# Gate and up of four feed-forward steps by one level of Strassen's algorithm, positions on partitions

## The chip, the core and the metric

The kernel runs on one core of one Trainium2 chip. The metric is the device time of one execution in microseconds (us). A core has TensorE (PE, matrix products, with its weight loads shown apart as PEld), VectorE (DVE), ScalarE (ACT), GpSimd (POOL) and SyncE (SP, which here only issues DMAs). Each engine works through its own instructions in order; they wait for one another on semaphores.

## The reference

Two layers of a decoder trunk on x of 512 positions by 1024 channels, all in float32. A layer is a feed-forward half step, a mixer, and a second feed-forward half step; a last norm ends it.

```python
def rmsnorm(x, g):                       # D_MODEL 1024, SEQ 512, D_FF 2816, DEPTH 2
    y = xf * lax.rsqrt(jnp.mean(xf * xf, axis=-1, keepdims=True) + RMS_EPS)
    return (y * g.astype(jnp.float32)).astype(x.dtype)
def swiglu(h, wg, wu, wd):
    return (jax.nn.silu(h @ wg) * (h @ wu)) @ wd
...
    for l in range(DEPTH):
        x = x + 0.5 * swiglu(rmsnorm(x, ffn1_norm[l]), ffn1_w_gate[l], ffn1_w_up[l], ffn1_w_down[l])
        x = x + hybrid_mixer(rmsnorm(x, mix_norm[l]), w_in[l], w_out[l], ...)
        x = x + 0.5 * swiglu(rmsnorm(x, ffn2_norm[l]), ffn2_w_gate[l], ffn2_w_up[l], ffn2_w_down[l])
    return rmsnorm(x, final_norm)
```

The mixer projects the normed x to 6168 columns, runs an mLSTM, a state-space scan and a convolution module on them, and projects 2048 columns back. Its computation is the same in both kernels.

## The kernel before

Activations lie with channels on partitions: x is eight tiles `xT` of 128 channels by 512 positions. A float32 product is made of three float32r passes. Each operand is split into a high part (a cast on ScalarE) and a low part (operand minus high part, on VectorE), and TensorE multiplies high by high, high by low and low by high. For weights this is `split_w` (L138; cast L145, difference L146, 128x1024 at a time, three buffers `whi` and three `wlo`), for activations `split_a` (L149; L151, L152). The normed input is the split pair `xh`, `xl` (eight tiles each), with the gain in it; the statistic R (one over the root of the mean square, a row of 512 repeated on all partitions) is multiplied in afterwards.

A feed-forward step `ffn` (L270) goes through its 2816 hidden columns in six groups, the first of 256 columns and five of 512. In a group each tile of 128 columns of gate, then of up, is a `proj` (L163): eight channel tiles by three passes, 24 matmuls with the weights stationary and 512 positions moving. An evicting chain follows: gate times R (L286), SiLU (L287), up times R (L288), their product (L289), and `split_a`. After the group's two or four hidden tiles, `contraction` (L236) multiplies them with the rows of the down weights into eight tiles of 128 channels, each added to `xT` (L263). In its first two output tiles the last hidden tile's part comes last.

Weights come by DMAs on SP's queue into three `raw` buffers of 1 MB (`stream`, L127). Mixers and feed-forward steps keep their own buffers at the same time. The order of each engine's instructions is set by a scheduler that takes them by priority, which is the place in the program's text; `shifted` moves a piece earlier or later in it (`early`: weights' loads and splits 100 steps ahead). Within an engine, what stands earlier is done earlier, whether or not what stands behind it could go first.

Between phases, `Norm.finish` (L216) makes R: column sums by TensorE (L188), root on ScalarE (L173), reciprocal on VectorE (L174), four transposes on TensorE (L181) and a copy (L220). In the first phase of all, R and the first products come from code of its own. The last contraction of the kernel is in `Final` (from L851), with positions on partitions; it transposes `xT` by L867.

## Time and profile before

| | us |
|---|---|
| median of 3 runs | 2321.57 (2321.07 to 2323.57) |
| span of the profiled execution | 2319.0 |
| TensorE busy in it | 2300.8 (99%) |
| VectorE busy | 1434.7 (62%) |
| ScalarE busy | 957.4 (41%) |
| moved by DMA | 224.64 MB, 97 GB/s |

The profiled execution's own device time is not listed apart from its span; the median of the runs is 2.6 us above that span, and this is taken as what lies around it. Matmuls overlap in the records: one lasts 0.39 us there, but the next starts some 0.23 us later, and this spacing is what a matmul costs while TensorE has no other wait. The same holds in a smaller measure on VectorE, where an instruction of 1.22 us lets the next begin after 1.14 us.

### The profile page before, as it was taken

How to read it: one execution, taken by the hardware profiler on the slowest of the kernel's cores; microseconds unless marked ns; L12 is line 12 of the kernel's file. 1: busy time of each engine (PE TensorE's matmuls, PEld its weight loads, DVE VectorE, ACT ScalarE, POOL GpSimd, SP SyncE). 2: the span in 40 equal slices, each digit the busy share in tenths (PEclk: the TensorE clock that was granted, in tenths of full speed). 3: DMA queues.
4: the chain of work that ended last, by engine and by line, in shares of the span. 5: the costliest groups of instructions: out<-in, count | busy, mean ns of one | idle time of the engine just before them, and what ended most of it. 6: DMA issues, size and time to landing. Idle time of an engine off the chain costs nothing.

```text
span 2319.0 us, 26273 instructions
## 1 busy us (share of the span) xinstructions
PE 2300.8 (99%) x10499; PEld 1893.0 (82%) x10499; DVE 1434.7 (62%) x2085; ACT 957.4 (41%) x1449; POOL 83.3 (4%) x145
## 2 busy tenths in 40 slices
PE   8999999999999999999999999999999999999998
PEld 7888888788888888888888888878888888888887
DVE  5444447999957654444554444489998586544445
ACT  5222225756555532222332222266666554222223
POOL 0000000010110000000000000000101000000000
PEclk9999999999999999999999999999999999999999
DMA  5232232333322322332323233323333323223231
GB/s 165 92 109 92 94 106 76 109 91 109 95 95 81 108 91 86 97 109 76 107 91 109 76 107 98 102 75 110 110 98 106 94 70 110 91 91 104 79 109 55
DMA packets 186010, 224.64 MB, mean 97 GB/s; under 512 B 5625, under 2 KB 147353, under 8 KB 185889
## 3 DMA queue, kind: packets, MB, share of 16 engines
q1 hardware_dynamic: 179712, 208.68, 28.4%
q0 software_dynamic: 5088, 13.14, 1.9%
q8 instruction: 82, 1.34, 0.2%
q10 hardware_dynamic: 1088, 1.16, 0.1%
q14 instruction: 40, 0.32, 0.0%
HBM read 220.77 MB, written 2.19 MB: 96 GB/s over the span
## 4 chain that ended last, share of the span: by engine, by line
PE 95%; ACT 1%; issue 1%; DVE 1%; POOL 1%; DMA 0%; SPq 0%; POOLq 0%; ACTq 0%
PE pacc L159 27%; PE pacc L161 27%; PE pacc L160 27%; PE pacc L699 2%; PE pacc L700 2%; PE pacc L701 2%; PE pmix L661 1%; PE pmix L550 1%; PE pmix L563 0%; PE pmix L642 0%; PE pmix L664 0%; DMA raw<-in_x_dram 0%; POOL rb L539 0%; ACT L466 0%; PE pmix L769 0%
## 5 line engine op out<-in xcount | busy, mean ns | idle before, releaser
L145 ACT CAST whi<-raw 128x1024 fp32r<-128x1024 f32 (+1 forms) x396 | 413.1, 1044 | 1094.3 <-PE pacc L160 835.7
L159 PE MATMUL pacc<-xh,whi 128*128 128x512 f32 x1888 | 748.5, 397 | 0.0
L161 PE MATMUL pacc<-xh,wlo 128*128 128x512 f32 x1888 | 741.1, 393 | 0.0
L160 PE MATMUL pacc<-xl,whi 128*128 128x512 f32 x1888 | 736.9, 391 | 0.0
L146 DVE TENSOR_TENSOR wlo<-raw,whi 128x1024 fp32r<-128x1024 f32 (+1 forms) x396 | 479.8, 1212 | 119.9 <-ACT whi L145 109.4
L161 PEld LDWEIGHTS pacc<-xh,wlo 128*128 128x128 f32 x1888 | 354.5, 188 | 80.4 <-DVE wlo L146 0.4
L160 PEld LDWEIGHTS pacc<-xl,whi 128*128 128x128 f32 x1888 | 354.6, 188 | 78.0 <-DVE xl L229 0.5
L159 PEld LDWEIGHTS pacc<-xh,whi 128*128 128x128 f32 x1888 | 354.9, 188 | 71.9
L159 PE MATMUL pacc<-atile,whi 128*128 128x512 f32 x928 | 362.2, 392 | 0.0
L160 PE MATMUL pacc<-atile,whi 128*128 128x512 f32 x928 | 361.7, 390 | 0.0
L161 PE MATMUL pacc<-atile,wlo 128*128 128x512 f32 x928 | 361.6, 390 | 0.0
L288 DVE TENSOR_TENSOR tmp<-pacc,R 128x512 f32<-128x512 f32 x87 | 60.1, 691 | 278.0 <-PE pacc L161 278.0
L263 DVE SCALAR_TENSOR_TENSOR xT<-pacc,xT 128x512 f32<-128x512 f32 x184 | 125.8, 691 | 169.1 <-PE pacc L161 169.1
L159 PEld LDWEIGHTS pacc<-atile,whi 128*128 128x128 f32 x928 | 174.0, 188 | 37.2 <-ACT atile L151 1.5
L161 PEld LDWEIGHTS pacc<-atile,wlo 128*128 128x128 f32 x928 | 174.2, 188 | 36.5
L160 PEld LDWEIGHTS pacc<-atile,whi 128*128 128x128 f32 x928 | 174.4, 188 | 36.0
L286 DVE TENSOR_TENSOR tmp<-pacc,R 128x512 f32<-128x512 f32 x88 | 60.8, 691 | 210.1 <-PE pacc L161 210.1
L512 DVE SCALAR_TENSOR_TENSOR cacc<-upad,pA,cacc 128x512 f32<-128x512 f32 x240 | 175.6, 766 | 1.1
L465 DVE SCALAR_TENSOR_TENSOR mtile<-pacc,pB,mtile 128x511 f32<-128x511 f32 x144 | 106.8, 742 | 2.2 <-ACT mtile L463 2.2
L699 PE MATMUL pacc<-whi,xh 128*128 128x512 f32 x256 | 101.6, 398 | 0.8 <-DVE mtile L465 0.8
L700 PE MATMUL pacc<-wlo,xh 128*128 128x512 f32 x256 | 101.6, 397 | 0.0
L701 PE MATMUL pacc<-whi,xl 128*128 128x512 f32 x256 | 100.6, 395 | 0.0
(282 smaller groups left out, 1772.8 us busy)
## 6 DMA issues: line engine op xcount, KB each, us to landing
raw<-in_ffn_w_down_dram SPq DMA_DIRECT2D x44, 1024.0 KB, 5.0
raw<-in_ffn_w_gate_dram SPq DMA_DIRECT2D x43, 1024.0 KB, 5.3
raw<-in_ffn_w_up_dram SPq DMA_DIRECT2D x43, 1024.0 KB, 5.3
raw<-in_w_in_dram SPq DMA_DIRECT2D x40, 1024.0 KB, 5.4
raw<-in_w_out_dram SPq DMA_DIRECT2D x10, 1024.0 KB, 5.0
raw<-in_w_in_dram SPq DMA_DIRECT2D x16, 512.0 KB, 4.2
rb<-ssd_rows POOLq DMA_DIRECT2D x32, 256.0 KB, 4.3
raw<-in_w_out_dram SPq DMA_DIRECT2D x8, 512.0 KB, 4.0
```

The lines of the kernel that those rows point to most:

```text
L145: nc.scalar.copy(hv, v)
L146: nc.vector.tensor_tensor(lv, v, hv.bitcast(F32), op=sub)
L159: nc.tensor.matmul(ps, wh, ah, start=start and k == 0, stop=False)
L160: nc.tensor.matmul(ps, wh, al, start=False, stop=False)
L161: nc.tensor.matmul(ps, wl, ah, start=False, stop=stop and k == n - 1)
L263: nc.vector.scalar_tensor_tensor(xT[d], ps, scale, xT[d], op0=mul, op1=add)
L286: nc.vector.tensor_tensor(a, pg, nrm.R, op=mul)
L465: nc.vector.scalar_tensor_tensor(o[:, d:], ps[:, 0:S - d], w[3 - d], o[:, d:], op0=mul, op1=add)
L512: nc.vector.scalar_tensor_tensor(o, u[:, j:j + S], col(cA, j * 4 + c), o, op0=mul, op1=add)
L699: nc.tensor.matmul(pv[c], xh[k][:, cs(c)], hv[:, k2, :], start=k == 0, stop=False)
L700: nc.tensor.matmul(pv[c], xh[k][:, cs(c)], lv[:, k2, :], start=False, stop=False)
L701: nc.tensor.matmul(pv[c], xl[k][:, cs(c)], hv[:, k2, :], start=False, stop=k == KT - 1)
```

## The change

The first group of each feed-forward step stays as it was. The five groups of 512 columns, 20 in the four steps, are made by `gated` (L333 of the new file). Gate and up of 512 columns by 512 positions over 1024 channels are seen as one product of two-by-two blocks: positions in halves of 256, channels in halves of 512, and gate and up as the two column blocks. One level of Strassen's algorithm in Winograd's form makes it from seven block products instead of eight. They are called "11", "5", "12", "6", "7", "3" and "22" in the code. A product is 24 matmuls: two tiles of 128 positions, four channel tiles, three passes. Now a piece of 128 positions is stationary and 512 weight columns move, so that results lie with positions on partitions.

The sums of input blocks that four of the products need (a5, a6, a7, a3) are made once a step in `Norm.combine` (L255): eight scalings by the gain, sixteen sums of 256 columns, four casts and four differences. In the first phase it stands behind the first group's tiles, in the other three ahead of them. The sums of weight blocks are made in place by `plus` (L361), four pairs of 128x1024 additions a block on VectorE. Fourteen `split_w` of 128x1024 are made a block, where there were eight. Partial sums are put together on VectorE (L393, L394, L400, L405, L411), the statistic comes in as a column `nr` per position (L386, L406, L412, L413), and the four results (the sign turned, hence the factor -0.5 in the contraction) are transposed on TensorE, 16 times 128x128 a block (L418), into four PSUM tiles that `split_a` splits (L181, L182).

The halves of the next block's product "11" stand ahead of and behind the transposes, in place of the first product's tile. In the last group of a step, half of the contraction of the group before is held back to stand there. Loads of gate and up are half tiles of 512 KB in six buffers; only one quarter of gate comes as a 1 MB tile. `SOON` takes evictions 200 steps earlier in the priorities. Buffers of mixers and feed-forward steps are now opened per phase, and share memory. TensorE's matmuls in the whole program go from 10002 to 9838: 480 fewer of 512 columns, 320 more transposes, 4 fewer elsewhere.

```diff
+SOON = 200
...
+    def half():
+        return mp_.tile([P, 1024], F32, tag="half", name="half", bufs=6)
+    def halves(src):
+        out = []
+        for j in range(2):
+            with shifted(-early[0]):
+                v = half().rearrange("p (k n) -> p k n", n=512)
+                nc.sync.dma_start(v, src[:, 2 * j:2 * j + 2, :])
+                out.append(v)
+        return out
...
+        def combine(self):
+            self.comb = []
+            for k in range(KT // 2):
+                lo = mp_.tile([P, 1024], F32R, tag="c", name="clo", bufs=8)
+                hi = mp_.tile([P, 1024], F32R, tag="c", name="chi", bufs=8)
+                g1, g2 = tmp(), tmp()
+                nc.vector.tensor_scalar(g1, xT[k], self.g[:, k:k + 1], None, op0=mul)
+                nc.vector.tensor_scalar(g2, xT[k + 4], self.g[:, k + 4:k + 5], None, op0=mul)
+                a, b, c, d = g1[:, 0:256], g1[:, 256:512], g2[:, 0:256], g2[:, 256:512]
+                t = half()
+                a5, a6, a7, a3 = [t[:, i * 256:(i + 1) * 256] for i in range(4)]
+                nc.vector.tensor_tensor(a5, d, b, op=sub)
+                nc.vector.scalar_tensor_tensor(a6, a5, -1.0, a, op0=mul, op1=sub)
+                nc.vector.tensor_tensor(a7, a, b, op=sub)
+                nc.vector.scalar_tensor_tensor(a3, a6, -1.0, c, op0=mul, op1=sub)
+                nc.scalar.copy(hi, t)
+                nc.vector.tensor_tensor(lo, t, hi.bitcast(F32), op=sub)
+                self.comb.append((hi, lo))
+        def left(self, name, k, t):
+            if name in ("11", "12", "22"):
+                c = (name[0] == "2") * 256 + t * P
+                k += (name[1] == "2") * 4
+                return xh[k][:, c:c + P], xl[k][:, c:c + P]
+            c = ("5", "6", "7", "3").index(name) * 256 + t * P
+            return [v[:, c:c + P] for v in self.comb[k]]
...
         def contraction(acts, wrows, scale, nxt):
...
+                if o + q == 0:
                     pss = [pacc() for _ in tiles[0:2]]
-                    for part in (slice(0, nk - 1), slice(nk - 1, nk)):
+                    for part in (slice(0, max(nk - 2, 1)), slice(max(nk - 2, 1), nk)):
                         for ps, terms in zip(pss, tiles):
                             mm3(ps, terms[part], part.start == 0, part.stop == nk)
...
+    def gated(nrm, wg, wu, c0, acts):
+        g1 = halves(wg[:, 0:4, c0:c0 + 512])
+        def product(left, right, ps, start=True):
+            for _ in product_halves(left, right, ps, start):
+                pass
+        def product_halves(left, right, ps, start=True):
+            more = dict(skip_group_check=not start)
+            split = [split_w(v) for v in right]
+            order = ((0, 0), (0, 1), (1, 0), (1, 1)) if left != "22" else ((0, 0), (1, 0), (0, 1), (1, 1))
+            for n, (j, t) in enumerate(order):
+                    if n == 2:
+                        yield
+                    hv, lv = split[j]
+                    for i in range(2):
+                        k = 2 * j + i
+                        ah, al = nrm.left(left, k, t)
+                        nc.tensor.matmul(ps[t], ah, hv[:, i, :], start=start and k == 0, stop=False, **more)
+                        nc.tensor.matmul(ps[t], ah, lv[:, i, :], start=False, stop=False, **more)
+                        nc.tensor.matmul(ps[t], al, hv[:, i, :], start=False, stop=k == 3, **more)
+        def plus(a, b):
+            with shifted(-early[0]):
+                for v, w in zip(a, b):
+                    nc.vector.tensor_tensor(v, v, w, op=add)
+        r = nrm.r
+        two = range(2)
+        A = [pacc() for _ in two]
+        first = product_halves("11", g1, A)
+        yield next(first)
+        u1 = halves(wu[:, 0:4, c0:c0 + 512])
+        g2 = stream(wg[:, 4:8, c0:c0 + 512], 4, 512)
+        g2 = [g2[:, 0:2, :], g2[:, 2:4, :]]
+        u2 = halves(wu[:, 4:8, c0:c0 + 512])
+        for _ in first:
+            pass
+        u = [mp_.tile([P, S], F32, tag="u", name="u", bufs=3) for _ in two]
+        with shifted(-SOON):
+            for t in two:
+                nc.scalar.copy(u[t], A[t])
+        yield
+        plus(g1, u1)
+        C = [pacc() for _ in two]
+        product("5", g1, C)
+        product("12", g2, A, start=False)
+        gate = [tmp() for _ in two]
+        with shifted(-SOON):
+            for t in two:
+                nc.scalar.activation(gate[t], A[t], AF.Silu, scale=r[:, t:t + 1])
+        plus(g1, u2)
+        B = [pmix() for _ in two]
+        product("6", g1, B)
+        w = [tmp() for _ in two]
+        with shifted(-SOON):
+            for t in two:
+                nc.vector.tensor_tensor(u[t], B[t], u[t], op=add)
+                nc.vector.tensor_tensor(w[t], C[t], u[t], op=add)
+        plus(u1, u2)
+        E = [pacc() for _ in two]
+        product("7", u1, E)
+        with shifted(-SOON):
+            for t in two:
+                nc.vector.tensor_tensor(w[t], E[t], w[t], op=add)
+        product("3", u2, C, start=False)
+        act = [tmp() for _ in two] + w
+        with shifted(-SOON):
+            for t in two:
+                nc.vector.tensor_tensor(act[t], C[t], u[t], op=add)
+                nc.vector.scalar_tensor_tensor(act[t], act[t], r[:, t:t + 1], gate[t], op0=mul, op1=mul)
+        plus(g1, g2)
+        product("22", g1, E, start=False)
+        with shifted(-SOON):
+            for t in two:
+                nc.vector.tensor_tensor(u[t], E[t], u[t], op=add)
+                nc.scalar.activation(u[t], u[t], AF.Silu, scale=r[:, 2 + t:3 + t])
+                nc.vector.scalar_tensor_tensor(w[t], w[t], r[:, 2 + t:3 + t], u[t], op0=mul, op1=mul)
+        yield
+        for m in range(4):
+            ps = pmix()
+            for c in range(NCH):
+                nc.tensor.transpose(ps[:, c * P:(c + 1) * P], act[c][:, m * P:(m + 1) * P], ident)
+            with shifted(-SOON):
+                acts.append(split_a(ps))
+        yield
     def ffn(nrm, wg, wu, wd, nxt, side=iter(()), pair=None, ready=(), final=None):
...
         ready = list(ready)
...
         wg = wg.rearrange("(k p) f -> p k f", p=P)
         wu = wu.rearrange("(k p) f -> p k f", p=P)
...
+        blocks = [([], f) for f in range(256, dff, 512)]
+        blocks = [(gated(nrm, wg, wu, f, acts), acts, f) for acts, f in blocks]
+        for gi in range(len(blocks) + 1):
+            last = gi == len(blocks)
+            if gi == 0:
+                acts, f0 = [], 0
+                vg, vu = pair or [stream(w[:, :, 0:256], KT, 256) for w in (wg, wu)]
+                ahead = not ready
+                if ahead:
+                    nrm.combine()
                 for m in range(2):
                     pg, pu = ready.pop(0) if ready else (proj(vg, m), proj(vu, m))
                     a, b = tmp(), tmp()
...
+                    with shifted(-SOON):
+                        nc.vector.tensor_tensor(a, pg, nrm.R, op=mul)
+                        nc.scalar.activation(a, a, AF.Silu)
+                        nc.vector.tensor_tensor(b, pu, nrm.R, op=mul)
+                        nc.vector.tensor_tensor(a, a, b, op=mul)
+                        acts.append(split_a(a))
+                early[0] = EARLY
+            else:
+                steps, acts, f0 = blocks[gi - 1]
+                next(steps)
+            if last:
+                for _ in held:
+                    pass
+            else:
+                next(blocks[gi][0])
+            if gi:
+                if last and final:
+                    final.gather()
+                next(steps)
+            if gi == 0 and not ahead:
+                nrm.combine()
+            if not last:
+                next(blocks[gi][0])
             next(side, None)
...
+            after = nxt() if nxt and last else None
+            sign = 0.5 if gi == 0 else -0.5
+            if last and final:
+                final.finish(acts, wd[f0:f0 + len(acts) * P, :], sign)
             else:
...
+                held = contraction(acts, [wd[f0:f0 + len(acts) * P, :]], sign, after)
+                if gi == len(blocks) - 1 and not final:
+                    next(held)
+                    next(held)
+                else:
+                    for _ in held:
+                        pass
         return after
```

Three places on VectorE show how the order moves. The first is a group in the middle of the first step, from the last eviction of a gate and up pair to the contraction; `wlo_1596` is of the down weights. Before:

```order
L289 TENSOR_TENSOR tmp_1511<-tmp_1511,tmp_1512 128x512 [waits DVE_49,Activation_49]
L146 TENSOR_TENSOR wlo_1596<-raw_1593,whi_1595 128x1024 [waits DMAHW2_49,Activation_49]
L152 TENSOR_TENSOR atile_1518<-tmp_1511,atile_1517 128x512 [waits Activation_49]
L286 TENSOR_TENSOR tmp_1579<-pacc_1525,R_320 128x512 [waits PE_49]
L146 TENSOR_TENSOR wlo_1628<-raw_1593,whi_1627 128x1024 [waits Activation_49]
L288 TENSOR_TENSOR tmp_1580<-pacc_1554,R_320 128x512 [waits PE_49]
L289 TENSOR_TENSOR tmp_1579<-tmp_1579,tmp_1580 128x512 [waits DVE_49,Activation_49]
L146 TENSOR_TENSOR wlo_1662<-raw_1659,whi_1661 128x1024 [waits DMAHW3_49,Activation_49]
```

After, at the end of product "22" of a block (its sums are `pacc_1145` and `pacc_1146`); `half_1259` and `half_1321` are the next block's weights of gate and up, `wlo_1266` and `wlo_1270` those of its product "11", `tmp_1138` the last of the four results that are transposed:

```order
L176 TENSOR_TENSOR wlo_1266<-half_1259,whi_1265 128x1024 [waits DMAHW5_49,Activation_49]
L411 TENSOR_TENSOR u_881<-pacc_1145,u_881 128x512 [waits PE_49]
L361 TENSOR_TENSOR half_1259<-half_1259,half_1321 128x1024 [waits DMAHW7_49,DVE_49]
L413 SCALAR_TENSOR_TENSOR tmp_1137<-tmp_1137,nr_321,u_881 128x512 [waits Activation_49]
L411 TENSOR_TENSOR u_882<-pacc_1146,u_882 128x512 [waits PE_49]
L176 TENSOR_TENSOR wlo_1270<-half_1261,whi_1269 128x1024 [waits DMAHW6_49,Activation_49]
L413 SCALAR_TENSOR_TENSOR tmp_1138<-tmp_1138,nr_321,u_882 128x512 [waits Activation_49]
L176 TENSOR_TENSOR wlo_1360<-raw_1357,whi_1359 128x1024 [waits DMAHW3_49]
L176 TENSOR_TENSOR wlo_1392<-raw_1357,whi_1391 128x1024 [waits Activation_49]
```

An addition of the next block's weights now stands between the evictions of the two halves of product "22", and waits for a DMA.

The second is the first phase, where its first group ends and its contraction's additions to `xT` begin. Before:

```order
L152 TENSOR_TENSOR atile_374<-tmp_367,atile_373 128x512
L288 TENSOR_TENSOR tmp_378<-pmix_247,R_320 128x512
L289 TENSOR_TENSOR tmp_377<-tmp_377,tmp_378 128x512
L146 TENSOR_TENSOR wlo_468<-raw_463,whi_467 128x1024
L152 TENSOR_TENSOR atile_384<-tmp_377,atile_383 128x512
L263 SCALAR_TENSOR_TENSOR xT0_91<-pacc_395,xT0_91 128x512
L263 SCALAR_TENSOR_TENSOR xT1_92<-pacc_396,xT1_92 128x512
L263 SCALAR_TENSOR_TENSOR xT2_93<-pacc_411,xT2_93 128x512
```

After, with `combine` (L264 to L274; `half_419` holds the first channel tile's four sums):

```order
L264 TENSOR_SCALAR tmp_415<-xT0_88,g1_137 128x512
L447 TENSOR_TENSOR tmp_377<-tmp_377,tmp_378 128x512
L176 TENSOR_TENSOR wlo_496<-raw_493,whi_495 128x1024
L176 TENSOR_TENSOR wlo_532<-raw_493,whi_531 128x1024
L182 TENSOR_TENSOR atile_384<-tmp_377,atile_383 128x512
L265 TENSOR_SCALAR tmp_416<-xT4_92,g1_137 128x512
L271 TENSOR_TENSOR half_419<-tmp_415 128x256
L269 TENSOR_TENSOR half_419<-tmp_416,tmp_415 128x256
L264 TENSOR_SCALAR tmp_428<-xT1_89,g1_137 128x512
L270 SCALAR_TENSOR_TENSOR half_419<-half_419,tmp_415 128x256
L327 SCALAR_TENSOR_TENSOR xT0_88<-pacc_499,xT0_88 128x512
L327 SCALAR_TENSOR_TENSOR xT1_89<-pacc_500,xT1_89 128x512
```

The additions to `xT` and the first group's last eviction stand among `combine`'s instructions.

The third is the start of the second feed-forward step, from the last of the mixer's splits to the first eviction. Before:

```order
L206 SCALAR_TENSOR_TENSOR xl7_114<-xT7_98,pB_1167,xh7_106 128x512
L214 TENSOR_TENSOR ss_2588<-ss_2588,tmp_6087 128x512
L146 TENSOR_TENSOR wlo_6207<-raw_6107,whi_6206 128x1024
L174 RECIPROCAL rc_6096<-rc_6096 128x4
L146 TENSOR_TENSOR wlo_6250<-raw_6247,whi_6249 128x1024
L286 TENSOR_TENSOR tmp_6167<-pacc_6113,R_6090 128x512
```

After, where `nr_6341` is the statistic from which R is made:

```order
L264 TENSOR_SCALAR tmp_6400<-xT3_91,pB_1347 128x512
L272 SCALAR_TENSOR_TENSOR half_6391<-half_6391,tmp_6388 128x256
L265 TENSOR_SCALAR tmp_6401<-xT7_95,pB_1347 128x512
L271 TENSOR_TENSOR half_6404<-tmp_6400 128x256
L269 TENSOR_TENSOR half_6404<-tmp_6401,tmp_6400 128x256
L205 RECIPROCAL nr_6341<-nr_6341 128x4
L270 SCALAR_TENSOR_TENSOR half_6404<-half_6404,tmp_6400 128x256
L274 TENSOR_TENSOR clo_6385<-half_6391,chi_6386 128x1024
L444 TENSOR_TENSOR tmp_6469<-pacc_6415,R_6340 128x512
```

The reciprocal and the first eviction (L444) stand behind most of `combine`.

## Rows read from the trace of the kernel before

**Rows 1.** The page's part 1 (busy us, share, xinstructions) and part 4 (chain's shares).
```profile
PE 2300.8 (99%) x10499; PEld 1893.0 (82%) x10499; DVE 1434.7 (62%) x2085; ACT 957.4 (41%) x1449; POOL 83.3 (4%) x145
...
PE 95%; ACT 1%; issue 1%; DVE 1%; POOL 1%; DMA 0%; SPq 0%; POOLq 0%; ACTq 0%
```

**Rows 2.** The timeline of TensorE in a feed-forward group: start us, us, engine, line, op.
```profile
199.90 0.39 PE L161 MATMUL pacc<-xh,wlo 128*128 128x512 f32 x1
...
202.65 0.39 PE L161 MATMUL pacc<-xh,wlo 128*128 128x512 f32 x1
...
211.58 0.39 PE L161 MATMUL pacc<-xh,wlo 128*128 128x512 f32 x1
```

**Rows 3.** The timeline of TensorE in a mixer projection with positions on partitions.
```profile
660.07 0.40 PE L701 MATMUL pacc<-whi,xl 128*128 128x512 f32 x1
...
671.97 0.39 PE L701 MATMUL pacc<-whi,xl 128*128 128x512 f32 x1
```

**Rows 4.** The timeline of VectorE in a contraction of four tiles: xT's additions 2 and 5.
```profile
236.34 0.69 DVE L263 SCALAR_TENSOR_TENSOR xT<-pacc,xT 128x512 f32<-128x512 f32 x1 [2.03 <-PE pacc L161]
...
244.50 0.69 DVE L263 SCALAR_TENSOR_TENSOR xT<-pacc,xT 128x512 f32<-128x512 f32 x1 [0.63 <-PE pacc L161]
```

**Rows 5.** The timeline of TensorE at the transposes of the last phase.
```profile
2254.09 2.78 PE L867 MATMUL pmix<-ident,xT 128*128 128x128 f32 x24
2256.63 0.48 PE L159 MATMUL pacc<-xh,whi 128*128 128x512 f32 x1
```

**Rows 6.** The same line's instructions: min/median/max ns of one.
```profile
L867 PE MATMUL pmix<-ident,xT x32: 270/272/273, 2254.1 to 2258.4; 128*128 128x128 f32 x32
```

**Rows 7.** The timeline of VectorE in a feed-forward group.
```profile
203.08 0.69 DVE L288 TENSOR_TENSOR tmp<-pacc,R 128x512 f32<-128x512 f32 x1 [3.36 <-PE pacc L161]
203.87 0.70 DVE L289 TENSOR_TENSOR tmp<-tmp 128x512 f32<-128x512 f32 x1
204.48 1.22 DVE L146 TENSOR_TENSOR wlo<-raw,whi 128x1024 fp32r<-128x1024 f32 x1
205.62 0.68 DVE L152 TENSOR_TENSOR atile<-tmp,atile 128x512 fp32r<-128x512 f32 x1
```

**Rows 8.** The timeline of ScalarE in the same group.
```profile
208.40 1.06 ACT L145 CAST whi<-raw 128x1024 fp32r<-128x1024 f32 x1 [3.17 <-PE pacc L160]
209.35 0.63 ACT L287 ACTIVATE tmp<-tmp 128x512 f32<-128x512 f32 x1
```

**Rows 9.** The DMA view's issues: KB each, median us to landing.
```profile
raw<-in_ffn_w_gate_dram SPq DMA_DIRECT2D x43, 1024.0 KB, 5.3
...
raw<-in_w_in_dram SPq DMA_DIRECT2D x16, 512.0 KB, 4.2
...
raw<-in_ffn_w_gate_dram SPq DMA_DIRECT2D x2, 512.0 KB, 9.0
```

**Rows 10.** The timeline of VectorE at the first phase's first groups.
```profile
38.23 0.69 DVE L288 TENSOR_TENSOR tmp<-pmix,R 128x512 f32<-128x512 f32 x1 [2.12 <-PE pmix L967]
...
54.87 0.69 DVE L286 TENSOR_TENSOR tmp<-pacc,R 128x512 f32<-128x512 f32 x1 [3.37 <-PE pacc L161]
```

**Rows 11.** One line's instructions, at a scaling by a column: min/median/max ns.
```profile
L915 DVE TENSOR_SCALAR tmp<-tmp,fr x4: 476/482/488, 2308.4 to 2314.9; 128x512 f32<-128x512 f32 x4
```

**Rows 12.** The same for an operation of 256 columns.
```profile
L647 DVE TENSOR_TENSOR wide<-wide,et x16: 412/418/423, 464.3 to 1775.4; 128x256 f32<-128x256 f32 x16
```

**Rows 13.** The timeline of VectorE at the second phase's beginning.
```profile
799.13 0.69 DVE L261 TENSOR_TENSOR xT<-pacc,xT 128x512 f32<-128x512 f32 x1 [0.68 <-PE pacc L161]
...
810.07 0.18 DVE L174 RECIPROCAL rc<-rc 128x4 f32<-128x4 f32 x1 [3.30 <-ACT rc L173]
```

**Rows 14.** What TensorE waited for: us in total, times, longest.
```profile
PE pacc L952 <- DMA raw<-in_x_dram: 2.9, 1, 2.9
```

**Rows 15.** Busy time (xinstructions) of the engines by stretch, PEclk, DMA share, GB/s.
```profile
12.00:16.00 4.00, 4.00 (x19) 3.50 (x19) 2.10 (x3) 2.97 (x10) 0.00 (x0) 0.63 1.17 310
...
200.00:300.00 100.00, 100.00 (x439) 81.95 (x438) 46.99 (x56) 26.64 (x32) 0.54 (x1) 1.00 0.30 96
```

More of the change, by code (lines that the diff above doesn't have):

```diff
@@ L54, in trunk, with __call__, tile @@
     tp = ctx.enter_context(tc.tile_pool(name="tp", bufs=1))
-    mp_ = ctx.enter_context(tc.tile_pool(name="mp", bufs=1))
+    class Phase:
+        @contextmanager
+        def __call__(self, name):
+            with tc.tile_pool(name=name, bufs=1) as self.pool:
+                yield
+        def tile(self, *args, **kwargs):
+            return self.pool.tile(*args, **kwargs)
+    mp_ = Phase()
     dr = ctx.enter_context(tc.tile_pool(name="dr", bufs=1, space=DRAM))
@@ L168, in proj, with rstd_cols @@
         return ps
-    def rstd_cols(ps, n, eps):
-        r = tp.tile([P, NCH], F32, tag="rc", name="rc", bufs=4)
+    def rstd_cols(ps, n, eps, r=None):
+        if r is None:
+            r = tp.tile([P, NCH], F32, tag="rc", name="rc", bufs=4)
         nc.scalar.activation(r, ps, AF.Sqrt, bias=eps, scale=1.0 / n)
@@ L196, in __init__ @@
             self.sums = None
-            self.ss = mp_.tile([P, S], F32, tag="ss", name="ss", bufs=1)
+            self.ss = tp.tile([P, S], F32, tag="ss", name="ss", bufs=1)
         def prep(self, k):
@@ L216, in finish @@
         def finish(self):
-            self.R = mp_.tile([P, S], F32, tag="R", name="R", bufs=1)
+            self.R = tp.tile([P, S], F32, tag="R", name="R", bufs=1)
             with shifted(AFTER):
-                r = stat(self.ss, D, eps_r) if self.sums is None else rstd_cols(self.sums, D, eps_r)
-                nc.scalar.copy(self.R, rows(r))
-            return self
+                self.r = tp.tile([P, NCH], F32, tag="nr", name="nr", bufs=2)
+                stat(self.ss, D, eps_r, self.r) if self.sums is None else rstd_cols(self.sums, D, eps_r, self.r)
+                nc.scalar.copy(self.R, rows(self.r))
+            return self
+        def combine(self):
[23 more added lines that the diff above has]
+            return [v[:, c:c + P] for v in self.comb[k]]
         def apply(self):
@@ L851, in trunk, with gather @@
     class Final:
-        def __init__(self):
-            self.g = [mp_.tile([P, S], F32, tag="rb", name="fg", bufs=4) for _ in range(2)]
+        def gather(self):
+            o = [mp_.tile([P, 1024], F32, tag="c", name="fo", bufs=8) for _ in range(NCH + 1)]
+            *o, self.g = [[t[:, q * S:(q + 1) * S] for q in range(2)] for t in o]
+            self.o = [list(t) for t in zip(*o)]
             for q, g in enumerate(self.g):
@@ L858, in __init__ @@
                 nc.gpsimd.dma_start(g, row.partition_broadcast(P))
-        def gather(self):
-            self.o = [[mtile() for _ in range(NCH)] for _ in range(2)]
             for q in range(2):
@@ L922, in trunk @@
     x = I["x"].rearrange("b (c p) d -> p (b c) d", p=P)
-    vs = [mp_.tile([P, 2 * MH * (P + 1)], F32, tag="xv", name="x0", bufs=2)[:, 0:1024] for _ in range(2)]
+    scope = ExitStack()
+    scope.enter_context(mp_("ff0"))
+    vs = [half(), half()]
     v = wp.tile([P, 2048], F32, tag="raw", name="raw", bufs=3)
@@ L1030, in trunk @@
     for l in range(depth):
-        if l:
-            nrm.finish()
-        nrm = ffn(nrm, I["ffn1_w_gate"][l], I["ffn1_w_up"][l], I["ffn1_w_down"][l], lambda: Norm(gain(l, 3)),
-                  load_params(0) if l == 0 else iter(()), *([pair, zip(ready[0::2], ready[1::2])] if l == 0 else []))
-        nxt = Norm(gain(l, 4))
-        nrm.finish()
-        mixer(l, nrm, pars[l], nxt)
-        w2 = [I["ffn2_w_" + n][l] for n in ("gate", "up", "down")]
-        if l + 1 < depth:
-            nrm = ffn(nxt.finish(), *w2, lambda: Norm(gain(l + 1, 2)), load_params(l + 1))
-        else:
-            ffn(nxt.finish(), *w2, None, final=Final())
+        with scope if l == 0 else mp_(f"ff{2 * l}"):
+            if l:
+                nrm.finish()
+            nrm = ffn(nrm, I["ffn1_w_gate"][l], I["ffn1_w_up"][l], I["ffn1_w_down"][l], lambda: Norm(gain(l, 3)),
+                      load_params(0) if l == 0 else iter(()),
+                      *([pair, zip(ready[0::2], ready[1::2])] if l == 0 else []))
+        with mp_(f"mix{l}"):
+            nxt = Norm(gain(l, 4))
+            nrm.finish()
+            mixer(l, nrm, pars[l], nxt)
+        w2 = [I["ffn2_w_" + n][l] for n in ("gate", "up", "down")]
+        with mp_(f"ff{2 * l + 1}"):
+            nxt.finish()
+            if l + 1 < depth:
+                nrm = ffn(nxt, *w2, lambda: Norm(gain(l + 1, 2)), load_params(l + 1))
+            else:
+                ffn(nxt, *w2, None, final=Final())
 _INS = ['x', 'ffn1_norm', 'ffn1_w_gate', 'ffn1_w_up', 'ffn1_w_down', 'mix_norm', 'w_in', 'w_out',
```

34 lines of the change are left out of this document (8 added, 26 removed).

## The prediction

> **What bounds the kernel now.** I read first the busy times and the chain of waits [rows 1]: TensorE is busy 2300.8 of 2319.0 us and makes 95% of the chain, VectorE 62%, ScalarE 41%. So a matmul less is worth its spacing, and a wait that is put on TensorE costs its whole length. Then I took the spacings from the timelines. In a feed-forward group the starts from 199.90 to 211.58 span 51 matmuls [rows 2], 0.2290 us each. In a mixer projection with positions stationary and 512 weight columns moving, the form of the new products, 660.07 to 671.97 is again 51 matmuls [rows 3], 0.2333 each. In a contraction three additions to xT apart are 244.50 - 236.34 = 8.16 us for 72 matmuls [rows 4], 0.2267 each. The 24 transposes from 2254.09 leave TensorE to the next matmul at 2256.63 [rows 5], 0.106 each, though a record of one lasts 0.272 [rows 6].
>
> On VectorE a 128x1024 operation takes 1.14 us to the next start (204.48 to 205.62), a 512-column one 0.61 (203.87 to 204.48), and an eviction starts 0.20 us after its tile's last matmul has left its slot (202.65 + 0.23 to 203.08) [rows 2, 7]. On ScalarE a cast of 128x1024 takes 1.06 and a SiLU 0.63 [rows 8]. In a steady stretch of 100 us VectorE is busy 47, DMA a share of 0.30 [rows 15]: there is room, and the question is where the new work queues.
>
> **The matmuls.** 480 go, at 0.2290: -109.9 us. The 3360 that stay in the products change their form. The 1440 in "11", "12" and "22" have xh and xl stationary as in rows 3: 1440 x (0.2333 - 0.2290) = +6.2. The 1920 in "5", "6", "7" and "3" have slices of the combined tiles stationary, which no row shows; I take 0.2300, between rows 4 and rows 3 and next to rows 2, for +1.9. All at 0.2267 would be -7.7, all at 0.2333 +14.4. Sum taken: +8.1.
>
> **The transposes.** 320 at the 0.106 of rows 5 add 33.9. That is their price where they stand ready; the ends are 0.106 and 0.272. I take the spacing because the 24 of rows 5 follow one another in the same way, into PSUM tiles that VectorE and ScalarE empty.
>
> [...]
>
> **The steady block.** VectorE's work a block is 22 operations of 128x1024 (14 splits, 8 additions) and 4 more splits for the down weights, 26 x 1.14 = 29.6, and some 26 of 512 columns (14 on the partial sums, 4 of the transposed tiles, 8 additions to xT), 15.9: 46 us. TensorE's block is 168 x 0.2314 + 96 x 0.2267 + 1.7 = 62.3. So it fits on the average. In the order's first place it does not fit at one point. The transposes need the last result, which needs VectorE's L411 and L413 and a SiLU for the second half of product "22". Ahead of L411 for that half stands the addition to the next block's weights, which waits for a DMA of up weights. On SP that DMA is queued behind the load into the buffer that the last split for "22" must leave; and that split waits for a wlo buffer that product "3" gives back in its middle. Counted from that middle: cast 1.06, difference 1.14 and 0.3 us between them make 2.5; issue some 0.4; two halves of 512 KB, together the bytes of a 1 MB load, 5.3 [rows 9]; the addition can start at 8.2 and ends at 9.4. Product "22"'s second half is done at 2.8 + 5.6 + 0.2 = 8.6. Behind the addition come L413 of the first half, L411 of the second (to 10.7), the SiLU (to 11.4), a split that VectorE has begun meanwhile (to 11.8) and the last L413 (to 12.5). TensorE, after half a product "11" and two transposes, wants this at 11.5. So it waits 1.0 us in each of 16 blocks (the last of each step has its contraction held back as cover): +16. With a landing in 4.2, as 512 KB have in a mixer [rows 9], the wait is 0; with the 9.0 of the first loads it is 4.7 each, +75.
>
> **The first step's entry.** The 26 us of work that VectorE has from its eviction at 38.23 to the split for product "5" are 8 scalings at some 0.40 (482 ns each, less the overlap) [rows 11], 16 operations of 256 columns at some 0.36 [rows 12], 8 additions to xT at 0.61, nine operations of 1.14 and three of 0.61. In this time TensorE has a product "11" (5.6) and the first group's contraction (96 x 0.2267 / 2 = 10.9). It now begins its next tile about 54.87 - 5.7 = 49.2 [rows 10]; with product "11" ahead of it that is 54.7. VectorE is at 38.2 + 26 = 64.3 without gaps, and dependent operations (0.79 instead of 0.61 in rows 7) and a last cast take it to some 68. I take a wait of 13, bounds 9 and 17. Such an idle stretch costs clock: after the 2.9 us wait for x [rows 14] the granted clock was 0.63 in the stretch 12 to 16 us [rows 15], which is 1.5 us lost; I add 2.
>
> **The three other entries.** The reciprocal comes at 810.07, 10.9 us after the mixer's last addition [rows 13]. Now some 10 us of combine stand in VectorE's queue between, and TensorE's row of R stands at its old place. Walking the queues I get 2.2 us for R's transposes and 1.4 for the contraction that follows: 3.6 each, +10.8; bounds 5 and 16 in all.
>
> **The rest.** The last step's gather of xT and its first two splits stand closer together: +2, bounds 0 and 4. The mixers' instructions are the same, in an order that differs little; bounds -4 and +4, taken 0. The half-tile loads move the same bytes. ScalarE gets six more casts a block, 6.4 us of some 63, and is not on the path except as counted.
>
> **Sum.** 2319.0 - 109.9 + 8.1 + 33.9 + 16 + 13 + 2 + 10.8 + 2 = 2294.9; with the 2.6 us by which the runs' median lies above the span, 2297.5. I forecast 2298.
>
> **Rivals.**
> - *The queue in front of the transposes is the bound (slower).* One mechanism: the half load behind the addition lands later than 5.3 us after its issue, and each microsecond beyond that is one in each of 16 blocks. The gain of 23.6 us is gone at a landing of 6.8 us, 1.5 later. At the 9.0 of the first loads the time is 2298 + 59 = 2357. For it: six such loads stand close together behind one wait. Against: the DMA share is 0.30 on the average, and 9.0 was reached only while x and the first weights came at once [rows 9].
> - *Transposes cost their duration (slower).* 320 x (0.272 - 0.106) = +53: 2351. For it: they come in fours, each with its own wait for a PSUM tile. Against: rows 5.
> - *The products run at 0.2267 and the waits in the blocks vanish (faster by more).* -15.8 - 16, and the entries at their low ends, -9: 2257. For it: TensorE's contraction has that spacing already, and a landing of 4.2 us is enough. Against: rows 3.
> - *The gain is eaten in small pieces (no change).* All products at 0.2333, +6.3, and the entries at 17 and 16, +9, and 0.5 us more a block, +8: 2321.
>
> **How the numbers follow.** The forecast with its own range of 2284 to 2313: 0.50. Faster by more: 0.21. No change: 0.11. The queue: 0.11. Transposes at their duration: 0.07. The range that holds 8 in 10 reaches into the faster case to 2266 and into the slower ones to 2330. A difference under 0.2% (4.6 us: 2316.9 to 2326.2) can't be told from none by this measurement. Faster by more than that: the first two and a little of the third, 0.73; within it 0.10; slower, the last two less a little, 0.17.
>
> **What would show it.** In the profile after: a spacing of the L354 to L356 matmuls of 0.233 in "11", "12", "22" and less in "5", "6", "7", "3"; sixteen L418 transposes in 1.7 us when ready; in a steady block TensorE idle for about 1 us ahead of the third transpose, ended by VectorE's L413; idle of some 13 us ahead of product "5" near 55 us, ended by VectorE's L176, with a lower granted clock behind it; some 2 us ahead of R's transposes (L212) at three entries. TensorE's idle time in all would grow by some 40 us. It would be wrong if a block takes more than 65.7 us (8 x 24 x 0.2290 + 96 x 0.2267), if the idle in blocks is put down to loads of halves, or if transposes follow at 0.27.

## The result and the profile after

The changed kernel takes 2287.31 us (median of 4 runs, 2285.9 to 2288.57) against 2321.32 for the kernel before beside it: ratio 0.9854, 95% interval 0.984 to 0.9867. The forecast was 2298 with a range of 2266 to 2330. The profiled execution spans 2284.2 us, 34.8 less than before.

The page's busy times and chain, which answer to [rows 1]:

```profile
PE 2250.6 (99%) x10339; PEld 1836.7 (80%) x10339; DVE 1824.0 (80%) x2517; ACT 1126.3 (49%) x1633; POOL 83.0 (4%) x145
...
PE 92%; DVE 3%; ACT 2%; issue 1%; DMA 1%; POOL 0%; SPq 0%; POOLq 0%; ACTq 0%
```

TensorE is still the bound; VectorE rose from 62% to 80%. TensorE has 160 instructions fewer in the page (10499 and 10339): 480 products less and 320 transposes more, so none of the "4 fewer elsewhere" that were counted ahead of the prediction. TensorE's table of waits (us in total, times, longest) has four rows of over a microsecond that were not there before. Three are shown; the fourth, 1.2 us, is the gather of the last step:

```profile
PE pacc L354 <- ACT whi L175: 7.0, 1, 7.0
PE pmix L626 <- ACT atile L622: 4.6, 2, 3.2
PE pacc L189 <- DVE xT L327: 4.2, 6, 1.2
```

The first is the entry of the first step, the second the mLSTM gates in the two mixers, the third are tiles of contractions whose PSUM buffer VectorE gives back late (three in the first step, one in each other). No row names the transposes.

A steady block of the first step, from behind one row of transposes to behind the next, takes 63.0 us, where the prediction's walk gives 62.3 and a wait of 1.0, and its limit for being wrong is 65.7:

```profile
104.43 0.48 PE L354 MATMUL pacc<-whi,xh 128*128 128x512 f32 x1
...
167.44 0.48 PE L354 MATMUL pacc<-whi,xh 128*128 128x512 f32 x1
```

The spacing of the new products, from the first matmuls of their triples in a steady block (start us, us, engine, line, op):

```profile
149.68 0.39 PE L354 MATMUL pacc<-whi,chi 128*128 128x512 f32 x1
...
156.68 0.39 PE L354 MATMUL pacc<-whi,chi 128*128 128x512 f32 x1
...
157.38 0.39 PE L354 MATMUL pacc<-whi,xh 128*128 128x512 f32 x1
...
162.28 0.40 PE L354 MATMUL pacc<-whi,xh 128*128 128x512 f32 x1
```

Ten triples in 7.00 us and seven in 4.90: 0.2333 a matmul in both, the figure of [rows 3], where the forecast had 0.2300 for the combined tiles. The transposes stand at once behind, 16 in a row:

```profile
165.54 0.39 PE L356 MATMUL pacc<-whi,xl 128*128 128x512 f32 x1
165.78 1.91 PE L418 MATMUL pmix<-ident,tmp 128*128 128x128 f32 x16
```

The first begins 0.24 us after the matmul ahead of it, so TensorE did not wait. And VectorE around it, with SP's issues of the next block's halves:

```profile
160.66 0.68 DVE L411 TENSOR_TENSOR u<-pacc,u 128x512 f32<-128x512 f32 x1
161.26 1.21 DVE L361 TENSOR_TENSOR half<-half 128x1024 f32<-128x1024 f32 x1
162.39 0.75 DVE L413 SCALAR_TENSOR_TENSOR tmp<-tmp,nr,u 128x512 f32<-128x512 f32 x1
163.18 0.69 DVE L411 TENSOR_TENSOR u<-pacc,u 128x512 f32<-128x512 f32 x1
163.79 1.22 DVE L176 TENSOR_TENSOR wlo<-half,whi 128x1024 fp32r<-128x1024 f32 x1
164.93 0.75 DVE L413 SCALAR_TENSOR_TENSOR tmp<-tmp,nr,u 128x512 f32<-128x512 f32 x1
```

```profile
143.69 2.59 SPq L164 DMA_DIRECT2D half<-in_ffn_w_gate_dram  x2
149.44 8.04 SPq L164 DMA_DIRECT2D half<-in_ffn_w_up_dram  x4
```

The addition L361 has no bracket of idle time: its up half was issued at 149.44 and had landed long before 161.26, 3.7 us after its issue if it took the median of such loads. The last result ends at 165.68, 0.4 us before the fourth transpose needs it. The row of those loads (KB each, median us to landing):

```profile
half<-in_ffn_w_up_dram SPq DMA_DIRECT2D x80, 512.0 KB, 3.7
```

In the first step, the wait ahead of product "5" and the end of that product:

```profile
64.30 1.22 PE L354 MATMUL pacc<-whi,chi 128*128 128x512 f32 x2 [6.99 <-ACT whi L175]
...
71.97 0.39 PE L354 MATMUL pacc<-whi,xh 128*128 128x512 f32 x1
```

Its 24 matmuls take 7.67 us where 24 spacings of 0.2333 are 5.60, so they lose 2.1 us behind the wait.

The account of the 34.8 us, from this trace against that of before:

| term | forecast | measured |
|---|---|---|
| 480 matmuls gone, at 0.2290 | -109.9 | -109.9 |
| 3360 matmuls in the new form, 0.2333 for 0.2290 | +8.1 | +14.4 |
| 320 transposes, 0.106 forecast, 0.109 from one start to the next in the trace | +33.9 | +34.9 |
| wait ahead of the transposes, 16 blocks | +16 | 0 |
| first step: waits 10.6 (7.1 ahead of product "5", 3.5 in the contraction), slow matmuls behind them 2.1 | +13 +2 | +12.7 |
| three other entries | +10.8 | +2.7 |
| gather in the last step | +2 | +1.5 |
| gates in the mixers | 0 | +5.6 |
| the rest, by difference | 0 | +3.3 |
| sum | -24.1 | -34.8 |

The first two terms are counts times spacings, and so is that of the transposes: the sixteen above take 1.66 us and not 1.74, but the matmul behind them starts 0.03 us after the last one and then takes 0.32 itself, so 0.109 each is what they cost. The measured waits are start-to-start intervals less the usual spacing, so they are a little larger than the table of waits, which counts idle time. The rest was not taken apart; part of it is single spacings of 0.31 to 0.38 us for 0.23 in the blocks' contractions.

### The profile page after: what moved, and what is told of

Same layout as the page of the kernel before. It is cut to its first block, busy times and chain, and to the rows that moved or that the text cites. A ratio compares the mean times of both kernels' runs of the same rounds, so it can differ in the third digit from the quotient of the medians.

```text
span 2284.2 us, 26881 instructions
## 1 busy us (share of the span) xinstructions
PE 2250.6 (99%) x10339; PEld 1836.7 (80%) x10339; DVE 1824.0 (80%) x2517; ACT 1126.3 (49%) x1633; POOL 83.0 (4%) x145
## 4 chain that ended last, share of the span: by engine, by line
PE 92%; DVE 3%; ACT 2%; issue 1%; DMA 1%; POOL 0%; SPq 0%; POOLq 0%; ACTq 0%
PE pacc L189 14%; PE pacc L190 14%; PE pacc L191 14%; PE pacc L355 10%; PE pacc L354 10%; PE pacc L356 10%; PE pacc L877 3%; PE pacc L878 2%; PE pacc L879 2%; PE pmix L355 2%; PE pmix L354 2%; PE pmix L356 2%; PE pmix L418 1%; PE pmix L839 1%; DVE wlo L176 1%
## 5 line engine op out<-in xcount | busy, mean ns | idle before, releaser
L175 ACT CAST whi<-half 128x1024 fp32r<-128x1024 f32 x240 | 251.2, 1047 | 404.5 <-PE pacc L356 202.4
L176 DVE TENSOR_TENSOR wlo<-raw,whi 128x1024 fp32r<-128x1024 f32 (+1 forms) x276 | 332.5, 1206 | 119.2 <-ACT whi L175 112.8
L176 DVE TENSOR_TENSOR wlo<-half,whi 128x1024 fp32r<-128x1024 f32 x240 | 293.4, 1223 | 135.1 <-ACT whi L175 135.1
L189 PE MATMUL pacc<-xh,whi 128*128 128x512 f32 x608 | 243.8, 401 | 0.0
L191 PE MATMUL pacc<-xh,wlo 128*128 128x512 f32 x608 | 239.4, 394 | 0.0
L190 PE MATMUL pacc<-xl,whi 128*128 128x512 f32 x608 | 238.8, 393 | 0.0
L354 PE MATMUL pacc<-whi,chi 128*128 128x512 f32 x480 | 189.3, 396 | 7.0 <-ACT whi L175 7.0
L355 PE MATMUL pacc<-wlo,chi 128*128 128x512 f32 x480 | 192.3, 401 | 0.0
L356 PE MATMUL pacc<-whi,clo 128*128 128x512 f32 x480 | 188.6, 393 | 0.0
L361 DVE TENSOR_TENSOR half<-half 128x1024 f32<-128x1024 f32 x120 | 145.7, 1217 | 0.9
```

Source lines behind the costliest of these rows:

```text
L175: nc.scalar.copy(hv, v)
L176: nc.vector.tensor_tensor(lv, v, hv.bitcast(F32), op=sub)
L189: nc.tensor.matmul(ps, wh, ah, start=start and k == 0, stop=False)
L190: nc.tensor.matmul(ps, wh, al, start=False, stop=False)
L191: nc.tensor.matmul(ps, wl, ah, start=False, stop=stop and k == n - 1)
L354: nc.tensor.matmul(ps[t], ah, hv[:, i, :], start=start and k == 0, stop=False, **more)
```

## Experiments

Each ran beside the kernel before, whose median was 2322.0 to 2322.2 in these comparisons. The changed kernel itself was not run again beside them: where a time is set against its 2287.31, 2 or 3 us are within the spread of the runs.

**The spacing.** Why 0.2333 here and in [rows 3], but 0.2267 in contractions [rows 4]? One thing that differs is where the tiles lie: in the built programs the rows of `whi`, `wlo` and `atile` begin at multiples of 128 bytes in SBUF, those of `xh` and `xl` 64 bytes past one, those of `chi` and `clo` 32 past.

Edit of e1_comb, at the opening of each feed-forward phase:

```diff
+    mp_.tile([P, 24], F32, tag="pad", name="pad")
     vs = [half(), half()]
```

> The changed kernel with one edit: a pad of 96 bytes ahead of the buffers of each feed-forward phase, so that the rows of the combined tiles chi and clo begin at multiples of 128 bytes in SBUF (before this edit 32 bytes past one). Theory A, the address of an operand sets the spacing of matmuls: where stationary and moving tile both begin at such multiples (contractions) the trace shows 0.227 us, with xh or xl (64 bytes past) stationary 0.233, with chi or clo 0.2333 on the mean. Then the 1920 matmuls of products 5, 6, 7 and 3 go to 0.227, -12 us, to about 2275. Theory B, traffic of VectorE and ScalarE beside them, or the form (512 weight columns moving): nothing changes, 2287.

2275.55 us, ratio 0.9801 (0.9786 to 0.9815). In its trace the products with the combined tiles went to 0.2267 (ten triples in 6.80 us), and those with `xh` and `xl`, which the pad does not move, stayed at 0.2333 (ten in 7.00):

```profile
147.33 0.39 PE L354 MATMUL pacc<-whi,chi 128*128 128x512 f32 x1
...
154.13 0.39 PE L354 MATMUL pacc<-whi,chi 128*128 128x512 f32 x1
...
156.17 0.40 PE L354 MATMUL pacc<-whi,xh 128*128 128x512 f32 x1
...
163.17 0.40 PE L354 MATMUL pacc<-whi,xh 128*128 128x512 f32 x1
```

Edit of e2_align, in addition (the same edit alone, in the kernel before, is e3_before_align):

```diff
-    eps_r = const.tile([P, 1], F32, name="eps_r")
-    nc.vector.memset(eps_r, RMS_EPS)
-    eps_l = const.tile([P, 1], F32, name="eps_l")
-    nc.vector.memset(eps_l, LN_EPS)
     xT = [const.tile([P, S], F32, name=f"xT{k}") for k in range(KT)]
...
         nc.gpsimd.memset(t[:, 0:CK - 1], 0.0)
+    eps_r = ...
```

> As e1_comb, and the two small constants eps_r and eps_l stand behind the padded buffers instead of ahead of xT, so that xT, xh and xl too begin at multiples of 128 bytes. Theory A: 1440 matmuls of products 11, 12 and 22 and 768 of the mixers' projections with positions on partitions lose 0.006 us each, -13.5, and some 1800 that have xh or xl moving lose 0.0025 each, -4.5: about 2257. If only the stationary operand's address counts, 2262. Theory B: 2287.

2261.39 us, ratio 0.9742 (0.9725 to 0.9758).

> The kernel before with the constants moved in the same way, so that xh and xl begin at multiples of 128 bytes. Theory A: 768 matmuls with xh or xl stationary lose 0.006 us, -4.7, some 5600 with them moving lose 0.0019 (0.2290 to 0.227), -10.6: about 2306. If only the stationary operand counts, 2316. Theory B: 2321.

2304.83 us, ratio 0.9927 (0.9912 to 0.9942). The three came 0.6, 4.4 and 1.2 us from theory A; theory B and the form are out. e2_align's time alone lies nearer to the 2262 of "only the stationary operand"; e3_before_align, where that rival has 2316, rules it out. The timeline of e2_align, first matmuls of triples again:

```profile
148.04 0.39 PE L354 MATMUL pacc<-whi,chi 128*128 128x512 f32 x1
...
154.84 0.39 PE L354 MATMUL pacc<-whi,chi 128*128 128x512 f32 x1
155.52 0.39 PE L354 MATMUL pacc<-whi,xh 128*128 128x512 f32 x1
...
163.00 0.39 PE L354 MATMUL pacc<-whi,xh 128*128 128x512 f32 x1
```

Ten triples in 6.80 us, eleven in 7.48: 0.2267 in both. In e3_before_align 87 matmuls of a feed-forward group take 19.72 us, 0.2267 again, for the 0.2290 of [rows 2]:

```profile
194.91 0.39 PE L161 MATMUL pacc<-xh,wlo 128*128 128x512 f32 x1
...
214.63 0.39 PE L161 MATMUL pacc<-xh,wlo 128*128 128x512 f32 x1
```

So the change is worth 34.0 us as it stands, and 43.4 (2304.83 - 2261.39) where both kernels' operands are placed alike. The Trainium skill, "SBUF — State Buffer", section "Operand start alignment", says that a start at any multiple of the element size is legal, and that this is not about speed; here the speed differed, by 0.002 to 0.011 us a matmul.

**The entry of the first step.** Edit of e4_twelve, in every block:

```diff
+        product("12", g2, A, start=False)
         plus(g1, u1)
-        C = [pacc() for _ in two]
-        product("5", g1, C)
-        product("12", g2, A, start=False)
...
+        C = [pacc() for _ in two]
+        product("5", g1, C)
         plus(g1, u2)
```

> The changed kernel with product 12, which needs no sums of blocks, ahead of product 5 in every block. Theory: the 7.0 us wait ahead of product 5 in the first step is VectorE's queue of combine; 5.6 us of it are then covered, 2287 goes to about 2282, and the rest of TensorE's idle time is as it was. Rival: the wait stands on a late load of weights, or an equal wait appears in the other 19 blocks because the additions of weights now come beside other splits: no change, or slower by some us.

2280.89 us, ratio 0.9823 (0.9809 to 0.9838): the 6 us came, but not in the place that the theory named. The wait ahead of product "5" stayed:

```profile
PE pacc L354 <- ACT whi L175: 6.8, 1, 6.8
```

Product "12" filled the holes in the contraction instead: the row of waits for xT's additions (4.2 us, six times) is down to 0.4, once, and product "5" begins only 2.7 us later with 5.6 us of work more ahead of it. The queues of VectorE and ScalarE still set the time at which it can begin. That `combine` fills them is borne out by e8_all below: there `combine` stands elsewhere, and no wait is left ahead of product "5".

**The mixers' gates.** In the changed kernel's second mixer ScalarE's timeline shows why the gates come late:

```profile
1541.49 1.28 ACT L721 ACT_TABLE_LOAD   x1
1548.10 0.40 ACT L721 ACTIVATE rb<-rb,nlc 128x128 f32<-128x128 f32 x1 [5.32 <-POOL rb L718]
1548.52 1.28 ACT L644 ACT_TABLE_LOAD   x1
1549.81 0.63 ACT L644 ACTIVATE mtile<-mtile 128x512 f32<-128x512 f32 x1
1550.47 1.28 ACT L613 ACT_TABLE_LOAD   x1
1551.76 0.40 ACT L613 ACTIVATE atile<-atile,mc 4x128 f32<-4x128 f32 x1
```

An exponential of the scan waits 5.3 us for GpSimd, and the gates' exponentials (L613) stand behind it. In the kernel before, where the line is L435, the gates stood ahead:

```profile
1575.09 0.40 ACT L435 ACTIVATE atile<-atile,mc 4x128 f32<-4x128 f32 x1
...
1577.01 0.97 ACT L543 ACTIVATE rb<-rb,nlc 128x128 f32<-128x128 f32 x3
```

Edit of e5_gate:

```diff
-            nc.vector.tensor_scalar(nlc, lcs, -1.0, None, op0=mul)
...
             nc.vector.tensor_copy(ws, pe[:, 0:12].rearrange("p (c h) -> p c h", h=MH))
+            neg = tp.tile([P, NCH], F32, tag="rc", name="neg", bufs=4)[:, 0:1]
+            nc.vector.tensor_scalar(neg, en[:, 0, 0:1], 0.0, -1.0, op0=mul, op1=add)
+            nc.vector.tensor_scalar(nlc, lcs, neg, None, op0=mul)
```

> The changed kernel; in each mixer the column -cumsum that the exponentials of the scan's weights (line 721) read is made only when the mLSTM gates are done, so that ScalarE cannot stand at those exponentials ahead of the gates' own (line 613). Theory: the new waits of TensorE for the gates, 4.6 us by the table of waits and 5.6 by the spacing, come from ScalarE's queue, in which one exponential that waits for GpSimd was put ahead of the gates: they go, 2287 to about 2282. Rival: they come from the loads of the gates' bias rows, which the shared memory lets start only with the mixer: no change. Second rival: the exponentials come too late for the scan, and the wait only moves: no change or slower.

2282.68 us, ratio 0.983 (0.9814 to 0.9847), 4.6 less. The row of waits for the gates goes from 4.6 us to 0.4:

```profile
PE pmix L625 <- ACT atile L621: 0.4, 2, 0.2
```

The theory holds by this row; the difference in time by itself is little more than the spread. The first rival is out. Of the second a little is true: another wait of the mixers, for VectorE's `mtile`, rose from 0.3 to 1.5 us.

**The price of a transpose.** Edit of e6_dbl:

```diff
-            for c in range(NCH):
+            for c in range(2 * NCH):
+                c %= NCH
                 nc.tensor.transpose(ps[:, c * P:(c + 1) * P], act[c][:, m * P:(m + 1) * P], ident)
```

> The changed kernel with each of the 320 transposes of line 418 issued twice, into the same place. If a transpose costs its spacing of 0.109 us, +35, about 2322; if it costs its duration of 0.272 us, +87, about 2374; if transposes are hidden behind something that TensorE waits for anyway, less than +20.

2315.49 us, ratio 0.9972 (0.996 to 0.9984): 28.2 us for 320 more, 0.088 each, a little under the spacing and a third of the duration. The trace:

```profile
168.07 3.65 PE L419 MATMUL pmix<-ident,tmp 128*128 128x128 f32 x32
171.48 0.48 PE L354 MATMUL pacc<-whi,xh 128*128 128x512 f32 x1
```

Thirty-two hold TensorE for 3.41 us, where sixteen held it for 1.66 (165.78 to 167.44): 0.109 for each one more, the spacing. The time grew by less because other stretches became shorter: TensorE's waits for the mixers' gates went from 4.6 to 3.5 us and those for xT's additions from 4.2 to 3.4, among others.

The 275 ns of the Trainium skill's page "TensorE: Matmul & The Clock Gate", "Part 4: PE-mode transpose", agree with a record's duration (0.273 here) and are not what a transpose costs in a row of them.

**The chain ahead of the transposes.** Two kernels were to show how much slack it has. Edit of e7_extra, ahead of the first addition of weights, and of e9_chain, behind line 411:

```diff
+            nc.vector.tensor_tensor(g1[0], g1[0], g1[0], op=mx)
...
                 nc.vector.tensor_tensor(u[t], E[t], u[t], op=add)
+                nc.vector.tensor_tensor(u[t], u[t], u[t], op=mx)
```

> The changed kernel with one more 128x1024 operation on VectorE (the maximum of a tile with itself, 1.14 us) just ahead of the addition to the next block's weights that stands between the evictions of product 22. Theory: the queue ahead of the transposes has no slack left but costs nothing now, since loads land long before; then the last result comes 1.1 us later and TensorE waits some 0.7 to 1.1 us in each of 16 to 20 blocks, +11 to +22, about 2303. Rival: there is slack of more than a microsecond, the prediction's place was wrong altogether, and nothing changes: 2287 to 2290.

2289.27 us, ratio 0.9863 (0.9848 to 0.9877), 2.0 more, which is within the spread. It told nothing of slack: the scheduler put the new operation into the addition's place, and the addition behind the evictions.

> The changed kernel with one more operation of 512 columns on VectorE (the maximum of a tile with itself) between the eviction of each half of product 22 (line 411) and its SiLU. It cannot be taken out of the chain to the last result: 0.6 to 0.8 us more there for the second half, and as much for the first ahead of it. Theory: this chain ends just when TensorE comes to the last result (the wait is 0 only because the loads of the halves come 8 us early, and not because the chain is short): 0.7 to 1.5 us in each of 16 to 20 blocks, +11 to +28, about 2303. Rival: a slack of more than 1.5 us: 2287 to 2290.

2290.23 us, ratio 0.9859 (0.9842 to 0.9875), 2.9 more. Here the chain did grow: the last result is there 2.7 us after the first transpose. But the order changed with it:

```profile
168.62 1.47 PE L419 MATMUL pmix<-ident,tmp 128*128 128x128 f32 x12
169.84 0.48 PE L354 MATMUL pacc<-whi,xh 128*128 128x512 f32 x1
...
171.39 0.66 PE L419 MATMUL pmix<-ident,tmp 128*128 128x128 f32 x4
```

The scheduler issued twelve transposes, then five matmuls of the next product "11", then the four that need the late result; TensorE lost 0.3 us there. Neither the theory's 11 to 28 us nor a slack in the chain is what was found: for this length of chain the scheduler hid all but 0.3 us a block by another order. So no run shows how much a later last result costs in the old order.

**All together.** e8_all has the edits of e2_align, e4_twelve and e5_gate, and `combine` ahead of the first group in the first step too:

```diff
-                ahead = not ready
+                ahead = True
```

> All edits that helped, and one more: constants and combined tiles at multiples of 128 bytes, product 12 ahead of product 5, the gates ahead of the exponentials, and combine ahead of the first group also in the first step. If the terms add, 2261 - 6 - 5 = 2250, and combine's earlier place takes up to 8 off the first step's wait: 2242 to 2250. Rival: with combine ahead of the first group its evictions come late and the contraction waits instead: 2250 to 2256.

2242.05 us, ratio 0.9658 (0.9644 to 0.9672). The three edits alone would add to 2261.4 - 6.4 - 4.6 = 2250.4, so combine's place gives some 8 if the others add; it was not run alone. What is left of the first step's wait stands now ahead of product "11":

```profile
40.05 1.22 PE L354 MATMUL pacc<-whi,xh 128*128 128x512 f32 x2 [3.88 <-ACT whi L175]
42.34 0.80 PE L355 MATMUL pacc<-wlo,xh 128*128 128x512 f32 x1 [1.07 <-DVE wlo L176]
42.93 0.63 PE L356 MATMUL pacc<-whi,xl 128*128 128x512 f32 x1
43.35 0.63 PE L354 MATMUL pacc<-whi,xh 128*128 128x512 f32 x1
43.78 0.63 PE L355 MATMUL pacc<-wlo,xh 128*128 128x512 f32 x1
```

e10_late moved combine a little later in that step:

```diff
-                    nrm.combine()
+                    with shifted(60 if ready else 0):
+                        nrm.combine()
```

> As e8_all, with combine of the first step 60 places later in the priorities, so that the fourth of its casts on ScalarE stands behind the splits for product 12 and the copies of product 11's sums. Theory: e8_all's 5 us of waits in the first step (a cast of weights behind combine's casts) shrink by one cast, some 1 us: 2241. Rival: they stay with the other three casts, 2242.

2242.40 us, ratio 0.9656 (0.9642 to 0.967): the rival; the wait of 3.9 stayed.

## Why the prediction was right, and where its steps were wrong

The sign, the mechanism and the size of the two large terms were right: matmuls at their spacing less, transposes at their spacing more. The forecast was 11 us too high, and that it was no further off is in part luck. By the account above, four terms were 26.9 us too high (the blocks 16, the other entries 8.1, the first step 2.3, the gather 0.5) and four were 16.2 too low (the form 6.3, the gates 5.6, the rest 3.3, the transposes 1.0).

*The steady block* (16 forecast, 0 measured) failed at the sentence "On SP that DMA is queued behind the load into the buffer that the last split for '22' must leave". I gave the next block's halves the buffers in the order in which they had been taken. The trace has the gate halves issued at 143.69, when the splits for product "7" had read the first pair of up weights, and the up halves from 149.44, when those for product "3" had read the second. The load came eight microseconds earlier than the walk had it. The landing was too long as well: two halves were given 5.3 us, and one up half, which is all that this addition reads, landed in 3.7 (median). By the prediction's own words a landing in 4.2 leaves no wait, so putting either one right takes the term to nothing. The rest of that walk, chain and order, was what the trace shows, with 0.4 us to spare. All this is read from the trace; no run delayed the loads.

*The entries of the other steps* (10.8 forecast, 2.7 measured): the wait for R's transposes did not come at all; of the contraction's wait 0.7, 1.2 and 0.7 us came.

*The form of the matmuls* (8.1 forecast, 14.4 measured) lay at the upper bound: the combined tiles, for which no row stood, run like xh. The reason given, positions stationary and weights moving, was not the cause: with the tiles moved by some bytes the same form runs at 0.2267 (e1_comb, e2_align).

*The first step's entry* was right in cause and near in size (15 forecast, 12.7 measured), and right in place for two thirds of the wait: 7.1 us ahead of product "5", ended by ScalarE's cast of the summed weights and not, as the prediction had it, by VectorE's difference. The other 3.5 stood in the contraction ahead of it, ended by xT's additions. Then came the low clock. *The mixers* were not: "an order that differs little" hid 5.6 us, beyond the bound of 4, which e5_gate gives back as 4.6.

Of the signs named under "What would show it", sixteen transposes in 1.7 us came (1.66). A faster spacing with the combined tiles, idle ahead of the third transpose and idle ahead of R's transposes did not, and TensorE's idle time grew by 15.4 us (from 18.2 to 33.6) and not by some 40.

Of the rivals, transposes at their duration are out by e6_dbl. The queue ahead of the transposes did not decide, since the loads are early; what would happen with late loads was not tried. The faster rival had one half right, the waits in the blocks vanished; its other half, products at 0.2267, needs the other placement, and with it comes to 2261, near its 2257. Of the rival of small pieces the products at 0.2333 came true, and the long entries and blocks did not.

## What to carry to other kernels

A matmul and a transpose are priced by the spacing of their starts in the trace, in the same form and from the same tiles, and not by their records. Before a wait is forecast from a queue, find which buffer each load takes over, by who gives one back first; a wrong owner and a landing taken too long made a term of 16 us that did not come. A scheduler that keeps its own times may turn an unrelated part's order, so an unchanged phase needs its bounds as well.

## What the runs showed of the hardware

The spacing of 128x128x512 matmuls in three float32r passes depended on where their operands begin in SBUF. With both at multiples of 128 bytes it was 0.2267 us; with the stationary tile 64 bytes past such a multiple 0.2333; with the moving one 64 past 0.2290; with the stationary one 32 past 0.2316, 0.2376 and 0.2308 in the three passes. What lies behind it, and other offsets, were not tried. Two edits of a few bytes gave 25.9 us in the changed kernel, and the one of them that applies there gave 17.2 in the kernel before.

After the 7.0 us wait in the first step the granted clock was 0.50 in the stretch from 64 to 66 us (start and end, busy times, PEclk):

```profile
60.00:64.00 4.00, 0.00 (x0) 0.00 (x0) 3.25 (x3) 1.52 (x2) 0.00 (x0) 0.67 0.41 115
64.00:66.00 2.00, 1.67 (x3) 0.95 (x4) 1.97 (x3) 1.89 (x3) 0.00 (x0) 0.50 0.53 204
```

That is the lower of the two levels, 1.2 GHz. In e8_all, after waits of 3.9 and 1.1 us, matmuls followed one another at 0.43 us from 42.9 to 45.9, twice the spacing less a little.
